# Both parts of the activations in one matmul of 512 columns: a two-block transformer kernel on one core

## The chip, the cores and the metric

The program runs on one core of one Trainium2 chip. Time is device time in microseconds (us) of that core, from launch to end of one execution; lower is better. The engines have separate instruction queues that run in order and meet at semaphores: TensorE (PE for its matmuls, PEld for its weight loads), VectorE (DVE), ScalarE (ACT), GpSimd (POOL), and SyncE (SP), which issues the DMAs of the weights.

## The reference, cut to what matters

256 tokens `x` and 256 context tokens `ctx`, all of width 2048, go through two layers of a first block and one second block. All is fp32.

```python
# first block, layers l = 0, 1
hl = xl * (1.0 + sc_l) + sh_l                       # modulation; the same for the context
parts_l = jnp.split(hl @ w_in[l], SPLIT_POINTS, axis=-1)   # cu cb cc cg q k v ag pu pg
...                                                 # conv, differential attention, pooling: gated
out_l = concatenate([y_conv, y_attn, y_pool]) @ w_out[l]
xl = _layernorm(DEEPNORM_ALPHA * xl + g_l * out_l, ln_g[l], ln_b[l])
# in the last layer the context gives k and v alone

# second block, 256 tokens
h = rms_norm(x)           # @ w_in_2: qa ka va qb kb vb f ga gb
a = attention_a @ w_proj_a_2 * sigmoid(h @ w_ga) ; b = attention_b @ w_proj_b_2 * sigmoid(h @ w_gb)
x = x + (a + b) @ w_out_2
x = x + relu(rms_norm(x) @ w_up_2) ** 2 @ w_down_2  # width 8192; then a last norm
```

(The second block's lines are condensed to what the kernel computes.) The products are wanted in nearly fp32 precision, which is why the kernel does each of them in three matmuls.

## The kernel before, in words

**Three matmuls per product.** A weight tile and an activation tile are each split in two parts, a high part (`hi`, `ah`) that holds the leading bits and a low part (`lo`, `al`) that holds the rest. A product is hi·ah + hi·al + lo·ah, three matmuls that add up in one PSUM accumulator (`mm3`, L247 to L250).

**Two kinds of product.** `lin_b` (L252) keeps 128x128 pieces of the weights stationary and moves the activations: its output is [channel, token], with as many columns as there are tokens, 512 or 256. `lin_a` (L273) keeps activations stationary and moves the weights, mostly 512 columns at a time. In both, the work goes by chunks of 256 rows of k and 512 columns of the weights (two k tiles of 128 rows). A `lin_b` call has four accumulators `acc`, one per 128 channels, from a ring of five PSUM banks: in each chunk it goes through the four blocks, and in a block through the two k tiles. After the last chunk's matmuls of a block its `consume` function takes the accumulator out of PSUM (the eviction). A full call has 8 chunks; the two projections `w_proj_a_2` and `w_proj_b_2` have 4.

**Where 256 columns move.** `lin_b` runs on 256 tokens in layer 1 for q, ag, cu, cc, cb, cg, pu and pg (10 calls, q and ag twice), and in the second block for qa, ka, qb, kb (8 calls), the gates ga and gb (8), the projections (8 calls of 4 chunks) and w_up (16), and for the small forget gate f. Layer 0, the k of layer 1 and all of `lin_a` are of another form.

**Evictions.** Copies and activations of an accumulator run on ACT (`S.copy`, `S.activation`), products with an accumulator on DVE (`V.tensor_mul`). Those of w_up are longest: relu on ACT (L1166), square on POOL (L1167), then `split` (L318): the high part by ACT (L319), the low part by DVE (L320). At the projection b: product with the gate on DVE (L1143), sum on POOL (L1144), then `split`.

**The stream of weights.** `fetch` (L171) loads a chunk by a DMA from SP into `raw`, ACT writes the high part (L186), DVE subtracts for the low part (L187). There are three buffers of each of `raw`, `hi` and `lo`; two chunks are kept ready ahead of the one in use. Between the chunks a step of background work may run: attention of the heads that are ready, normalisation, and, up to layer 1, the modulation's sums on DVE (L386).

**The order of the instructions.** It is fixed when the program is built: a scheduler takes the program's statements, by its own estimates of their durations, and lays each engine's queue out; buffers come from small rings (four of `tmp`, five of `acc`), and an instruction waits when its ring buffer is not yet free.

`Act` holds the activations' parts in slots of 2048 columns, in before two tiles, `ah` and `al`.

Of the kernel before, what the change touches and what calls it, by code (L numbers as in the profile page):

```python
# [19 lines left out]
P = 128  # L20
# [42 lines left out]
def tile_two_blocks(ctx: ExitStack, tc: tile.TileContext, a: dict, out: bass.AP, blocks: dict):  # L63
    """blocks: takes, for each weight, its blocks in the order of their loads: (part, k tile, k tiles, column, columns)."""
# [6 lines left out]
    p_ah = pool("ah", 4)  # L71
    p_al = pool("al", 4)
# [66 lines left out]
    # An entry with a function is modulation: the function takes its tile as it comes. One with an engine is split there.  # L139
# [22 lines left out]
    def block(name, *where):  # L162
        """The next block of a weight: they lie in memory in the order of their loads, each partition's part in one run."""
# [33 lines left out]
    def side():  # L197
        """Modulation at the head of the stream."""
# [30 lines left out]
    def bg_step():  # L229
        """A step after every pace[0] chunks."""  # L230
# [42 lines left out]
    def lin_a(act, tiles, consume, korder=K16, mid=None, hold=1):  # L273
        """out[tok, n]: the activations stationary, the weights moving; the last chunks (hold) one token tile at a time."""
# [21 lines left out]

    class Act:
        """n activation tiles of w tokens, their two parts, in slots of 2048 columns."""

        def __init__(self, n, w):  # L300
            self.w, self.per = w, 2048 // w
            self.t = [(p_ah.tile([P, 2048], F32R, tag="ah", name="ah"), p_al.tile([P, 2048], F32R, tag="al", name="al"))
                      for _ in range(n // self.per)]

        def __getitem__(self, kt):
            j = (kt % self.per) * self.w
            return tuple(t[:, j:j + self.w] for t in self.t[kt // self.per])

        def block(self, kt, n, sl):
            """Tokens sl of n tiles from kt on."""  # L310
            j = (kt % self.per) * self.w
            return tuple(t[:, j:j + n * self.w].rearrange("p (k t) -> p k t", t=self.w)[:, :, sl]
                         for t in self.t[kt // self.per])
# [14 lines left out]
    def set_cols(l, which, kt, n, sums):  # L328
        """Shift (0) or scale (1) columns for n k tiles: scol[l][:, kt, stream, which]."""
# [4 lines left out]
    def mod_first(which, kt, n, tags=("aT",)):  # L334
        """Layer 0 on the tensor engine: sums over each quarter of k on its own quadrant, row s of it is stream s."""
# [35 lines left out]
    def mod_side(l, nt, streams=(0, 1), wait=5):  # L371
        """Sums on each partition by the side of the products, then over the partitions."""
# [47 lines left out]
    # column offsets in w_in  # L420
# [9 lines left out]
    # the column blocks of a product that the rows' statistics wait for: the last ones are short  # L430
# [860 lines left out]
```

## Time and profile before

| | |
|---|---|
| times of three runs | 2999.6, 2999.79, 3003.39 us (median 2999.79) |
| the profiled execution: span from the first to the last instruction | 3000.6 us |
| PE busy | 2926.6 us, 98% of the span, 17762 matmuls |
| PEld busy (weight loads, beside the matmuls) | 2547.9 us, 85% |
| DVE busy | 1878.3 us, 63% |
| ACT busy | 1233.4 us, 41% |
| POOL busy | 287.0 us, 10% |
| mean granted TensorE clock | 0.990 |
| weights and other data from HBM | 527.07 MB, 177 GB/s over the span |

The profiled execution's span lies within the three run times. A busy share is an average over stages with different limits; a matmul's recorded duration is longer than the spacing of matmuls, since they overlap in the array, so the spacing of their starts is what counts. Rows of the timeline give start, duration, engine, line, operation, and in brackets how long the engine was idle before and what ended that.

### The profile page before, as it was taken

How to read it: one execution, taken by the hardware profiler on the slowest of the kernel's cores; microseconds unless marked ns; L12 is line 12 of the kernel's file. 1: busy time of each engine (PE TensorE's matmuls, PEld its weight loads, DVE VectorE, ACT ScalarE, POOL GpSimd, SP SyncE). 2: the span in 40 equal slices, each digit the busy share in tenths (PEclk: the TensorE clock that was granted, in tenths of full speed). 3: DMA queues.
4: the chain of work that ended last, by engine and by line, in shares of the span. 5: the costliest groups of instructions: out<-in, count | busy, mean ns of one | idle time of the engine just before them, and what ended most of it. 6: DMA issues, size and time to landing. Idle time of an engine off the chain costs nothing.

```text
span 3000.6 us, 44450 instructions
## 1 busy us (share of the span) xinstructions
PE 2926.6 (98%) x17762; PEld 2547.9 (85%) x17762; DVE 1878.3 (63%) x2689; ACT 1233.4 (41%) x1792; POOL 287.0 (10%) x319
## 2 busy tenths in 40 slices
PE   8999999999999999999988999999999999999998
PEld 5677777778779788888877989999989989898997
DVE  3779987887985657467565464645555545555454
ACT  3123433432312446245434454744445434344444
POOL 0001001001100411021110000000101001010011
PEclk9999999999999999999998999999999999999999
DMA  8763345446664445445654545455555555555555
GB/s 304 264 205 130 128 160 172 137 144 198 227 202 131 130 140 171 157 157 171 228 174 134 184 146 193 141 190 183 183 190 175 190 190 182 195 186 189 190 183 169
DMA packets 156456, 534.22 MB, mean 178 GB/s; under 512 B 17860, under 2 KB 21196, under 8 KB 156248
## 3 DMA queue, kind: packets, MB, share of 16 engines
q1 hardware_dynamic: 148656, 510.79, 51.0%
q0 software_dynamic: 5632, 18.36, 2.0%
q8 instruction: 139, 2.28, 0.3%
q10 hardware_dynamic: 1960, 2.22, 0.3%
q14 instruction: 69, 0.57, 0.1%
HBM read 527.07 MB, written 4.23 MB: 177 GB/s over the span
## 4 chain that ended last, share of the span: by engine, by line
PE 68%; issue 6%; DVE 4%; ACT 1%; DMA 1%; POOL 0%; ACTq 0%; POOLq 0%; DVEq 0%
PE acc L248 22%; PE acc L250 22%; PE acc L249 22%; DVE lo L187 1%; PE aux L673 1%; DVE ma L386 0%; PE aux L641 0%; PE aux L663 0%; DMA mod<-in_w_mod_dram 0%; ACT hi L186 0%; PE aux L640 0%; DVE qs L627 0%; DMA tmp<-in_invc_dram 0%; PE aux L1060 0%; ACT L1125 0%
## 5 line engine op out<-in xcount | busy, mean ns | idle before, releaser
L187 DVE TENSOR_TENSOR lo<-raw,hi 128x1024 fp32r<-128x1024 f32 x766 | 948.6, 1240 | 845.4 <-ACT hi L186 842.9
L186 ACT CAST hi<-raw 128x1024 fp32r<-128x1024 f32 x769 | 805.4, 1049 | 1388.5 <-PE acc L249 784.6
L248 PE MATMUL acc<-ah,hi 128*128 128x256 f32 (+1 forms) x3856 | 1204.6, 313 | 2.5 <-ACT p L1125 1.5
L250 PE MATMUL acc<-ah,lo 128*128 128x256 f32 (+1 forms) x3856 | 1191.8, 309 | 3.1 <-DVE lo L187 2.9
L249 PE MATMUL acc<-al,hi 128*128 128x256 f32 (+1 forms) x3856 | 1191.3, 309 | 0.0
L248 PEld LDWEIGHTS acc<-ah,hi 128*128 128x128 f32 x3856 | 737.2, 191 | 63.6 <-issue 9.9
L250 PEld LDWEIGHTS acc<-ah,lo 128*128 128x128 f32 x3856 | 736.6, 191 | 44.2 <-issue 4.1
L249 PEld LDWEIGHTS acc<-al,hi 128*128 128x128 f32 x3856 | 737.6, 191 | 36.7 <-issue 3.0
L248 PE MATMUL acc<-hi,ah 128*128 128x512 f32 (+1 forms) x1568 | 583.1, 372 | 1.5 <-ACT ah L319 1.3
L250 PE MATMUL acc<-hi,al 128*128 128x512 f32 (+1 forms) x1568 | 578.5, 369 | 0.4 <-DVE al L320 0.4
L249 PE MATMUL acc<-lo,ah 128*128 128x512 f32 (+1 forms) x1568 | 578.6, 369 | 0.0
L386 DVE SCALAR_TENSOR_TENSOR ma<-mod,cc,ma 128x512 f32<-128x512 f32 x480 | 344.3, 755 | 30.7 <-DMA mod<-in_w_mod_dram 28.8
L248 PEld LDWEIGHTS acc<-hi,ah 128*128 128x128 f32 x1568 | 296.6, 189 | 54.0 <-issue 3.2
L250 PEld LDWEIGHTS acc<-hi,al 128*128 128x128 f32 x1568 | 296.5, 189 | 50.3 <-DVE al L320 1.1
L249 PEld LDWEIGHTS acc<-lo,ah 128*128 128x128 f32 x1568 | 296.8, 189 | 48.7 <-issue 0.5
L1167 POOL TENSOR_TENSOR tmp<-tmp 128x256 f32<-128x256 f32 x64 | 57.9, 914 | 579.6 <-ACT tmp L1166 579.6
L320 DVE TENSOR_TENSOR al<-tmp,ah 128x256 fp32r<-128x256 f32 (+1 forms) x96 | 65.0, 684 | 23.8 <-ACT ah L319 21.4
L649 ACT ACTIVATE pp<-aux,small 128x512 f32<-128x512 f32 (+1 forms) x96 | 58.3, 613 | 47.6 <-DVE small L645 47.5
L513 POOL TENSOR_TENSOR tmp<-p,cs 128x256 f32<-128x256 f32 x32 | 27.7, 877 | 508.4 <-DVE p L741 262.9
L124 POOL TENSOR_TENSOR small<-small,mhalf 128x1 f32<-128x1 f32 (+2 forms) x28 | 28.3, 1011 | 484.0 <-DVE small L680 251.8
L741 DVE TENSOR_TENSOR p<-acc,p 128x512 f32<-128x512 f32 x80 | 53.2, 686 | 29.5 <-PE acc L250 29.4
L319 ACT CAST ah<-tmp 128x256 fp32r<-128x256 f32 (+1 forms) x96 | 45.1, 478 | 60.0 <-POOL tmp L1167 35.3
(205 smaller groups left out, 1582.2 us busy)
## 6 DMA issues: line engine op xcount, KB each, us to landing
raw<-in_w_in_dram SPq DMA_DIRECT2D x384, 512.0 KB, 3.6
mod<-in_w_mod_dram SPq DMA_DIRECT2D x158, 512.0 KB, 4.3
raw<-in_w_up_dram SPq DMA_DIRECT2D x128, 512.0 KB, 3.3
raw<-in_w_down_dram SPq DMA_DIRECT2D x128, 512.0 KB, 3.5
raw<-in_w_out_dram SPq DMA_DIRECT2D x96, 512.0 KB, 4.4
mod<-in_w_mod_dram SPq DMA_DIRECT2D x68, 256.0 KB, 5.4
raw<-in_w_proj_a_dram SPq DMA_DIRECT2D x16, 512.0 KB, 3.2
raw<-in_w_proj_b_dram SPq DMA_DIRECT2D x16, 512.0 KB, 3.7
```

The source lines that it names most:

```text
L186: S.copy(hi, raw)
L187: (fn or V).tensor_sub(lo, raw, hi)
L248: mm(ps, lh, rh, start=start, stop=False)
L249: mm(ps, lh, rl, start=False, stop=False)
L250: mm(ps, ll, rh, start=False, stop=stop)
L319: S.copy(h, src)
L320: V.tensor_sub(lo, src, h)
L386: V.scalar_tensor_tensor(st[s], raw[:, kk, :], cc2[:, k, s:s + 1], st[s], op0=ALU.mult, op1=ALU.add)
L649: S.activation(t, ps[i][:, :nk], AF.Exp, bias=nm[:, i:i + 1], scale=QK_SCALE, accum_out=sums[:, i:i + 1])
L673: mm(po[:, o * P:(o + 1) * P], t[:, kt * P:(kt + 1) * P], vt[kt, g][:, hc * P:(hc + 1) * P], start=kt == 0, stop=kt == nk // P - 1)
L741: V.tensor_add(t, ps, t)
L1167: G.tensor_mul(t, t, t)
```

## The change

A `lin_b` call on 256 tokens joins the first two of the three matmuls: the stationary high part of the weights meets both parts of the activations at once, as 512 moving columns (256 of `ah`, then 256 of `al`), and writes them side by side into one PSUM bank of 512 columns. The third matmul, lo·ah, still has 256 columns and adds into the first half. So the accumulator holds two halves whose sum is wanted. `consume` gets a view that puts the two halves of a token next to each other, and the sum is formed on eviction by a DVE reduction of pairs: straight into the destination where a copy stood (`put`), else into a `tmp` tile on which the former operation then works (`val`). Both parts of the activations now lie in one tile, so that one access pattern reaches them. Calls on 512 tokens and `lin_a` stay as they were.

```diff
@@ lin_b
+        fold = 2 * ntok == 512
...
-                    mm3(p[:w, :ntok], hi[:, kk, c:c + w], lo[:, kk, c:c + w], ah[:, tok], al[:, tok],
-                        k0 == korder[0] and kk == 0, last and kk == nk - 1)
+                    start, stop = k0 == korder[0] and kk == 0, last and kk == nk - 1
+                    if fold:
+                        mm(p[:w, :].rearrange("p (a t) -> p a t", a=2), hi[:, kk, c:c + w], act.both(k0 + kk, tok),
+                           start=start, stop=False)
+                        mm(p[:w, :ntok], lo[:, kk, c:c + w], ah[:, tok], start=False, stop=stop)
+                    else:
+                        mm3(p[:w, :ntok], hi[:, kk, c:c + w], lo[:, kk, c:c + w], ah[:, tok], al[:, tok], start, stop)
                 if last:
-                    consume(c // P, p[:w, :ntok])
+                    consume(c // P, (p[:w].rearrange("p (a t) -> p t a", a=2),) if fold else p[:w, :ntok])
...
+    def put(t, ps):
+        if isinstance(ps, tuple):
+            V.reduce_sum(t, ps[0], axis=AX.X)
+        else:
+            S.copy(t, ps)
+    def val(ps):
+        if not isinstance(ps, tuple):
+            return ps
+        t = tmp(T)[:ps[0].shape[0]]
+        V.reduce_sum(t, ps[0], axis=AX.X)
+        return t
...
     class Act:
-            self.t = [(p_ah.tile([P, 2048], F32R, tag="ah", name="ah"), p_al.tile([P, 2048], F32R, tag="al", name="al"))
-                      for _ in range(n // self.per)]
+            self.t = [p_act.tile([P, 2, 2048], F32R, tag="act", name="act") for _ in range(n // self.per)]
...
+        def both(self, kt, tok):
+            j = (kt % self.per) * self.w
+            return self.t[kt // self.per][:, :, j + tok.start:j + tok.stop]
...
@@ evictions, three of them
-                S.copy(t, ps)
+                put(t, ps)
...
-            V.tensor_mul(t, ps, t)
+            V.tensor_mul(t, val(ps), t)
             G.tensor_add(t, t, sga[4 * j + b])
             split(mg[4 * j + b], t)
...
-                S.activation(t, ps, AF.Relu)
+                S.activation(t, val(ps), AF.Relu)
```

The built program shows it on two engines. First TensorE, at the start of a w_up call: the rows of its first block's two k tiles, before.

```order
L248 MATMUL acc_21329<-ah_20949,hi_21251 128x256
L249 MATMUL acc_21329<-al_20950,hi_21251 128x256
L250 MATMUL acc_21329<-ah_20949,lo_21252 128x256
L248 MATMUL acc_21329<-ah_20949,hi_21251 128x256
L249 MATMUL acc_21329<-al_20950,hi_21251 128x256
L250 MATMUL acc_21329<-ah_20949,lo_21252 128x256
```

The same call and block of the changed program, and the first tile of the next block.

```order
L267 MATMUL acc_19520<-act_19200,hi_19450 128x512
L269 MATMUL acc_19520<-act_19200,lo_19451 128x256
L267 MATMUL acc_19520<-act_19200,hi_19450 128x512
L269 MATMUL acc_19520<-act_19200,lo_19451 128x256
L267 MATMUL acc_19521<-act_19200,hi_19450 128x512
```

Six matmuls of 256 columns have become two of 512 and two of 256; over the program there are 2944 such pairs that became one matmul.

Second, VectorE at the end of the first w_up call, before: from the low part of the next call's second chunk (`lo_21282`) on.

```order
L187 TENSOR_TENSOR lo_21282<-raw_21279,hi_21281 128x1024
L320 TENSOR_TENSOR al_20990<-tmp_21291,ah_20989 128x256
L320 TENSOR_TENSOR al_20990<-tmp_21302,ah_20989 128x256
L187 TENSOR_TENSOR lo_21336<-raw_21333,hi_21335 128x1024
L320 TENSOR_TENSOR al_20990<-tmp_21313,ah_20989 128x256
L320 TENSOR_TENSOR al_20990<-tmp_21324,ah_20989 128x256
L187 TENSOR_TENSOR lo_21366<-raw_21363,hi_21365 128x1024
```

The same place of the changed program: `lo_19473`, `lo_19527` and `lo_19549` are the next call's second, third and fourth chunk.

```order
L315 TENSOR_REDUCE tmp_19481<-acc_19240 128x256
L186 TENSOR_TENSOR lo_19473<-raw_19470,hi_19472 128x1024
L315 TENSOR_REDUCE tmp_19492<-acc_19241 128x256
L340 TENSOR_TENSOR act_19238<-tmp_19480,act_19238 128x256
L315 TENSOR_REDUCE tmp_19503<-acc_19242 128x256
L186 TENSOR_TENSOR lo_19527<-raw_19524,hi_19526 128x1024
L340 TENSOR_TENSOR act_19238<-tmp_19491,act_19238 128x256
L315 TENSOR_REDUCE tmp_19514<-acc_19243 128x256
L340 TENSOR_TENSOR act_19238<-tmp_19502,act_19238 128x256
L186 TENSOR_TENSOR lo_19549<-raw_19546,hi_19548 128x1024
L340 TENSOR_TENSOR act_19238<-tmp_19513,act_19238 128x256
```

Four reductions stand between the weights' low parts and the activations' low parts, one per accumulator.

Third, VectorE at the end of the first call of projection b, before: products with the gate (L1143), low parts of the result (L320), and of the next call's second, third and fourth chunk (L187).

```order
L1143 TENSOR_TENSOR p32_18887<-acc_18911,p32_18887 128x256
L187 TENSOR_TENSOR lo_19008<-raw_19005,hi_19007 128x1024
L320 TENSOR_TENSOR al_18658<-p32_18887,ah_18657 128x256
L1143 TENSOR_TENSOR p32_18887<-acc_18912,p32_18887 128x256
L1143 TENSOR_TENSOR p32_18902<-acc_18913,p32_18902 128x256
L1143 TENSOR_TENSOR p32_18902<-acc_18914,p32_18902 128x256
L187 TENSOR_TENSOR lo_19058<-raw_19055,hi_19057 128x1024
L320 TENSOR_TENSOR al_18658<-p32_18887,ah_18657 128x256
L320 TENSOR_TENSOR al_18658<-p32_18902,ah_18657 128x256 x2
L187 TENSOR_TENSOR lo_19088<-raw_19085,hi_19087 128x1024
```

The same place of the changed program, where the product with the gate is L1166 and the low part of the third chunk is `lo_17549`.

```order
L315 TENSOR_REDUCE tmp_17506<-acc_17426 128x256
L186 TENSOR_TENSOR lo_17499<-raw_17496,hi_17498 128x1024
L1166 TENSOR_TENSOR p32_17400<-tmp_17506,p32_17400 128x256
L315 TENSOR_REDUCE tmp_17516<-acc_17427 128x256
L315 TENSOR_REDUCE tmp_17526<-acc_17428 128x256
L340 TENSOR_TENSOR act_17230<-p32_17400,act_17230 128x256
L1166 TENSOR_TENSOR p32_17400<-tmp_17516,p32_17400 128x256
L1166 TENSOR_TENSOR p32_17415<-tmp_17526,p32_17415 128x256
L315 TENSOR_REDUCE tmp_17536<-acc_17429 128x256
L340 TENSOR_TENSOR act_17230<-p32_17400,act_17230 128x256
L1166 TENSOR_TENSOR p32_17415<-tmp_17536,p32_17415 128x256
L186 TENSOR_TENSOR lo_17549<-raw_17546,hi_17548 128x1024
```

The third chunk's low part has moved from behind the last product and one low part of the result to behind the last product and two of them, with four reductions more ahead of it.

## Rows read from the trace of the kernel before

**Rows 1.** The page's part 1: busy time (share of the span) and instructions.
```profile
span 3000.6 us, 44450 instructions
PE 2926.6 (98%) x17762; PEld 2547.9 (85%) x17762; DVE 1878.3 (63%) x2689; ACT 1233.4 (41%) x1792; POOL 287.0 (10%) x319
```

**Rows 2.** Waits of PE, the longest first: total us, times, longest.
```profile
PE aux L983 <- ACT p L975: 13.0, 2, 9.3
PE aux L983 <- DVE small L813: 12.6, 1, 12.6
```

**Rows 3.** Groups of instructions, forms apart: xcount | busy us, mean ns.
```profile
L249 PE MATMUL acc<-al,hi 128*128 128x256 f32 x2944 | 835.0, 284 | 0.0
```

**Rows 4.** Timeline of PE, first and last of 51 matmuls in a row.
```profile
1999.92 0.28 PE L248 MATMUL acc<-ah,hi 128*128 128x256 f32 x1
...
2005.92 0.28 PE L250 MATMUL acc<-ah,lo 128*128 128x256 f32 x1
```

**Rows 5.** Timeline of PE in a `lin_a` call, first and last of 55 matmuls.
```profile
2419.59 0.39 PE L250 MATMUL acc<-hi,al 128*128 128x512 f32 x1
...
2431.82 0.39 PE L250 MATMUL acc<-hi,al 128*128 128x512 f32 x1
```

**Rows 6.** DVE reductions by line: xcount, ns min/median/max, first and last start, forms.
```profile
L642 DVE TENSOR_REDUCE small<-aux x96: 410/680/693, 284.6 to 1395.1; 128x1 f32<-128x512 f32 x64, 128x1 f32<-128x256 f32 x32
...
L361 DVE TENSOR_REDUCE small<-aux x8: 168/178/192, 16.1 to 224.7; 128x4 f32<-128x16 f32 x4, 128x8 f32<-128x32 f32 x4
```

**Rows 7.** Timeline of DVE in the attention of layer 1.
```profile
1122.32 1.29 DVE L642 TENSOR_REDUCE small<-aux 128x1 f32<-128x512 f32 x2
```

**Rows 8.** Timeline of DVE at the end of a projection b call.
```profile
2072.57 1.07 DVE L1143 TENSOR_TENSOR p<-acc,p 128x256 f32<-128x256 f32 x3
2073.57 1.31 DVE L187 TENSOR_TENSOR lo<-raw,hi 128x1024 fp32r<-128x1024 f32 x1
```

**Rows 9.** Timeline of ACT at the end of a w_up call.
```profile
2317.46 0.38 ACT L1166 ACTIVATE tmp<-acc 128x256 f32<-128x256 f32 x1
2318.07 0.39 ACT L1166 ACTIVATE tmp<-acc 128x256 f32<-128x256 f32 x1 [0.23 <-PE acc L250]
2319.31 0.41 ACT L319 CAST ah<-tmp 128x256 fp32r<-128x256 f32 x1 [0.86 <-POOL tmp L1167]
```

**Rows 10.** POOL and DVE steps behind evictions, by line, as in rows 6.
```profile
L1167 POOL TENSOR_TENSOR tmp<-tmp x64: 607/838/1369, 2294.9 to 2905.9; 128x256 f32<-128x256 f32 x64
...
L1144 POOL TENSOR_TENSOR p<-p,p x16: 737/1256/1722, 2070.1 to 2179.4; 128x256 f32<-128x256 f32 x16
...
L320 DVE TENSOR_TENSOR al<-tmp,ah x96: 424/552/1816, 21.0 to 2907.5; 128x256 fp32r<-128x256 f32 x64, 128x512 fp32r<-128x512 f32 x32
```

**Rows 11.** Timeline of DVE at the end of layer 1's first q call.
```profile
1102.77 0.45 DVE L511 STREAM_SHUFFLE tmp<-p 128x256 f32<-128x256 f32 x1
...
1103.46 1.31 DVE L512 TENSOR_TENSOR tmp<-tmp,cs 128x256 f32<-128x256 f32 x2
1104.70 0.75 DVE L514 TENSOR_TENSOR p<-tmp 128x256 f32<-128x256 f32 x2
```

**Rows 12.** Windows: us, busy PE PEld DVE ACT POOL, PEclk, DMA share, GB/s.
```profile
1104.00:1139.00 35.00, 32.07 (x216) 27.92 (x215) 33.50 (x47) 25.85 (x42) 10.82 (x9) 0.95 0.59 185
1139.00:1173.00 34.00, 31.95 (x226) 27.67 (x225) 29.98 (x53) 22.87 (x42) 6.04 (x3) 1.00 0.53 184
1319.00:1351.00 32.00, 29.97 (x209) 25.51 (x208) 31.45 (x47) 21.25 (x38) 11.04 (x8) 1.00 0.59 186
1351.00:1384.00 33.00, 30.92 (x228) 27.46 (x227) 29.61 (x53) 21.39 (x39) 4.89 (x5) 1.00 0.52 170
1885.00:1917.00 32.00, 31.83 (x257) 31.26 (x255) 22.20 (x63) 21.29 (x36) 0.00 (x0) 1.00 0.41 144
...
2300.00:2400.00 100.00, 100.00 (x700) 94.05 (x699) 51.75 (x52) 45.76 (x61) 11.06 (x13) 1.00 0.55 188
```

More of the change, by code (lines that the diff above doesn't have):

```diff
@@ L70, in tile_two_blocks @@
     p_wl = pool("wl", 3)
-    p_ah = pool("ah", 4)
-    p_al = pool("al", 4)
+    p_act = pool("act", 4)
     p32 = pool("p32", 20)
@@ L301, in __init__ @@
             self.w, self.per = w, 2048 // w
-            self.t = [(p_ah.tile([P, 2048], F32R, tag="ah", name="ah"), p_al.tile([P, 2048], F32R, tag="al", name="al"))
-                      for _ in range(n // self.per)]
+            self.t = [p_act.tile([P, 2, 2048], F32R, tag="act", name="act") for _ in range(n // self.per)]
         def __getitem__(self, kt):
             j = (kt % self.per) * self.w
-            return tuple(t[:, j:j + self.w] for t in self.t[kt // self.per])
-        def block(self, kt, n, sl):
+            t = self.t[kt // self.per]
+            return t[:, 0, j:j + self.w], t[:, 1, j:j + self.w]
+        def both(self, kt, tok):
             j = (kt % self.per) * self.w
-            return tuple(t[:, j:j + n * self.w].rearrange("p (k t) -> p k t", t=self.w)[:, :, sl]
-                         for t in self.t[kt // self.per])
+            return self.t[kt // self.per][:, :, j + tok.start:j + tok.stop]
     new_act = Act
@@ L533, in c @@
                 t = qt_[4 * g + b] = pair("q", 4 * g + b)
-                S.copy(t, ps)
+                put(t, ps)
                 rope(t[:, X] if both else t)
@@ L539, in c @@
             def c(b, ps):
-                S.activation(y_tile(4 + 4 * g + b), ps, AF.Silu)
+                S.activation(y_tile(4 + 4 * g + b), val(ps), AF.Silu)
             lin_b(hT, qs, c)
@@ L547, in c @@
             def c(b, ps):
-                S.copy(y_tile(b), ps)
+                put(y_tile(b), ps)
             lin_b(hT, qs, c)
@@ L553, in c @@
                 v = tmp(NT)
-                V.tensor_mul(v, ps, Y[b])
+                V.tensor_mul(v, val(ps), Y[b])
                 w = lambda i: smc("cw", l * 12 + b * 3 + i)
@@ L564, in c @@
             def c(b, ps):
-                V.tensor_mul(Y[b], ps, Y[b])
+                V.tensor_mul(Y[b], val(ps), Y[b])
             lin_b(hT, qs, c)
@@ L570, in c @@
                 s = tmp(NT)
-                S.activation(s, ps, AF.Silu)
+                S.activation(s, val(ps), AF.Silu)
                 G.tensor_mul(Y[b], Y[b], s)
@@ L582, in c @@
                 G.memset(u[:, :, 264:272], 0.0)
-                S.copy(u[:, :, 8:264], sh(ps))
+                if isinstance(ps, tuple):
+                    put(u[:, 0, 8:264], ps)
+                else:
+                    S.copy(u[:, :, 8:264], sh(ps))
                 w = WINDOWS[b]
@@ L608, in c @@
                 s = tmp(NT)
-                S.activation(s, ps, AF.Silu)
+                S.activation(s, val(ps), AF.Silu)
                 G.tensor_mul(Y[12 + b], Y[12 + b], s)
@@ L1007, in c @@
             if n[0] == "q":
-                S.activation(t, ps, AF.Copy, scale=HD_SCALE)
+                S.activation(t, val(ps), AF.Copy, scale=HD_SCALE)
             else:
-                S.copy(t, ps)
+                put(t, ps)
         lin_b(hn, TK, c)
@@ L1027, in c @@
             f, e, fone = tmp(T), tmp(T), tmp(T)
-            V.tensor_scalar(f[:NH], ps, sm[:NH, SM["bf"][0]:SM["bf"][1]], None, op0=ALU.add)
+            V.tensor_scalar(f[:NH], val(ps), sm[:NH, SM["bf"][0]:SM["bf"][1]], None, op0=ALU.add)
             S.activation(e[:NH], f[:NH], AF.Abs)
@@ L1124, in c @@
             sga[4 * j + b] = t = pair("sga", 4 * j + b)
-            S.activation(t, ps, AF.Sigmoid)
+            S.activation(t, val(ps), AF.Sigmoid)
         lin_b(hn, TK, c)
@@ L1128, in c @@
         def c(b, ps):
-            V.tensor_mul(sga[4 * j + b], ps, sga[4 * j + b])
+            V.tensor_mul(sga[4 * j + b], val(ps), sga[4 * j + b])
         lin_b(aA, TK, c, korder=K8)
@@ L1137, in c @@
             sgb[b] = pair("sgb", b)
-            S.activation(sgb[b], ps, AF.Sigmoid)
+            S.activation(sgb[b], val(ps), AF.Sigmoid)
         lin_b(hn, TK, c)
```

## The prediction

> **What bounds the kernel now.** I read the page's busy shares first, then PE's waits, then the spacing of matmul starts, and last the busy time of VectorE by stretches. PE is busy 98% of 3000.6 us [rows 1], and its longest waits belong to the two norms and last 13 us each [rows 2]. None is for an accumulator or a weight part, so in most of the program PE sets the pace and whatever shortens its stream shortens the run. The exceptions are the attention stretches of layer 1, where VectorE is busy 29.6 to 33.5 us of 32 to 35 while PE idles 2 to 3 us in each [rows 12]. Outside them, as in w_up and w_down, VectorE is busy 52% and PE all the time [rows 12].
>
> **What the change removes from PE.** A matmul's recorded length (284 ns at 256 columns [rows 3]) is not its price, since starts are closer. From the first to the last of 51 matmuls of 256 columns are 50 steps in 6.00 us, 120.0 ns each [rows 4]; from the first to the last of 55 of 512 columns are 54 steps in 12.23 us, 226.5 ns each [rows 5]. Two matmuls of 256 cost 240.0, one of 512 costs 226.5. The saving is 13.5 ns for each of 2944 pairs [rows 3], 39.7 us in all. (The forget gate has 16 pairs more, worth 0.2 us, which I leave out.) This is the whole gain. No row shows a moving operand in two pieces 8 KB apart. Its price lies between 226.5 (as one piece) and 240.0 (as two matmuls); I take 226.5, since the 512 columns stream into one bank as in the rows.
>
> The Trainium skill (TensorE: Matmul & The Clock Gate, Back-to-back issue gap) gives a warm gap of N/2.4 + 2.5 ns. By it, folding two matmuls would save 2.5 ns, 7.4 us in all, and not 39.7. The trace disagrees: both spacings exceed their columns' time at 2.4 GHz (106.7 and 213.3 ns) by 13.2 to 13.3 ns. I keep the measured steps; that the fold brings far less is a rival below.
>
> **What it adds to VectorE.** There are 50 calls with four evictions each, and one for f: 201 reductions, each of 512 inputs to 256 outputs. No row has this shape. By inputs, a reduction of 512 from PSUM takes 683 ns and one of 256 takes 410 [rows 6]; the lower end is 410, if pairs went at the rate of outputs. For the upper end, the small strided reductions go from 168 ns (16 inputs, 4 outputs) to 192 (32 and 8): 24 ns, of which 16 inputs at 1.07 ns (from 410 to 683 for 256) explain 17. So 7 ns go to 4 outputs; 256 outputs would add 0.46 us, giving 1.14. I take 0.68, the nearest in inputs. Back to back each takes less, 0.61 (two end within 1.29 us [rows 7]), and a product 0.33 (three in 1.00 us [rows 8]). That makes 123 us of new VectorE work. Nearly all lies beside PE, which must not be taken for free: the reduction waits for PE, the next chunks' low parts queue behind it on VectorE, and PE waits for those and for the freed accumulator. ACT loses 32 copies, which nobody waits for; the DMAs' order stays, and the faster chunk (2.77 us instead of 2.88) asks for 4% more than a DMA share of 0.55 [rows 12].
>
> **Deadlines at the end of a call.** Let t = 0 be the start of the last chunk. A block is two pairs of 226.5 + 120.0, so 0.69 us, and a chunk 2.77. A block's eviction may start about 0.2 us after its end (0.28 us of length against 0.12 of spacing, and the handoff). Of five accumulators the next call uses the spare first, so it needs the old blocks 0, 1 and 2 free at 3.46, 4.16 and 4.85. Its second, third and fourth chunk must be ready at 5.5, 8.3 and 11.1.
>
> *w_up* (16 calls). On VectorE: reduction 0 at 0.90, low part of chunk 2 (1.15 us net) at 1.51, reduction 1 at 2.66, done 3.34, in time for 4.16. Then the low part of the result, which waits for relu, square and high part: 0.38, about 0.95 (between 0.61 and 1.37) and 0.41 us, with handoffs, from 1.6 to 3.5 [rows 9, 10]. It ends at 3.9, so reduction 2 is done at 4.6, 0.25 us before its deadline. The chain of the next results runs on until 12; chunk 4's low part is ready at 10.4, needed at 11.1. I book nothing here, but the margin is 0.25 us.
>
> *q and k, quiet gates, projection a*: reductions 0 to 2 end at 1.6, 3.3 and 4.0 to 4.4. Nothing.
>
> *Projection b* (4 calls). In the new order the low part of chunk 3 stands behind four reductions, four products and two low parts that wait for POOL. Following it: product 0 at 2.66, reductions 1 and 2 at 3.0 and 3.6, low part 0 at 4.85 (POOL's sum takes 1.26 [rows 10]), products 1 and 2, reduction 3 at 5.9, low part 1 at 7.4, product 3 at 7.8, chunk 3 from 8.15 to 9.4. PE wants it at 8.3 plus one hi matmul, 8.5. That is 0.8 us late; L320 and L1144 stretch to 1.8 and 1.7 us where they run together [rows 10], so I take 1.2 (bounds 0 and 2.0): 4.8 us.
>
> The product with the gate has now both inputs in SBUF. The Trainium skill (SBUF — State Buffer, Who interferes with whom) says such a VectorE instruction and a GpSimd one that reads SBUF exclude each other for a whole instruction. By it the new product may wait out a sum of 1.26 us, an estimate that would put the four calls at 2.0 us each; no row has this pair, and the bound of 2.0 covers it.
>
> *Gates a under attention* (2 calls): VectorE is at 22.2 of 32 us [rows 12] with chains that wait for ACT, and 2.4 us more are due. I take 1.0 each (0 to 2): 2.0.
>
> *Layer 1* (10 calls). In each of the two stretches with ag and cu, and ag and cb, eight reductions add 4.9 us to a VectorE that has 5.5 and 3.9 us idle [rows 12], mostly in pieces too short to use. Bounds are 0 and 4.9; I take 3.0 each, 6.0. At q, a rotation stands between the reductions: after reduction 1 at 3.0 come product 0 (0.65), shuffle 1 (0.35), sum 0 (0.37) and product 1 (0.65) [rows 11], so reduction 2 starts at about 5.5, is done at 6.2, and its accumulator was due at 4.85: 1.3 us (0 to 2.3), twice 2.6. The four other calls get 0.6 each (0 to 1.5): 2.4. Together 11.0.
>
> **Sum.** 39.7 - 4.8 - 2.0 - 11.0 = 21.9 us less. Against the profiled span, 3000.6 - 21.9 = 2978.7; the median of the runs is 0.8 below that span, and from it comes 2977.9. I forecast 2978.
>
> **Rivals.** A measurement of this kernel can tell 0.2% (6.0 us) from no change.
>
> *All reductions hide.* Idle time on VectorE takes them up, as it does now in w_up: 2999.8 - 39.7 = 2960. Against it speak the filled attention stretches; for it, that three chunks of slack have absorbed delays so far.
>
> *The stalls eat the gain.* All upper bounds together (layer 1: 9.8 + 4.6 + 6.0, gates 4, projection b 8) make 32.4, so 2992.5; some w_up slips of 0.3 us bring it to about 2998, no change.
>
> *Pairs are slow on VectorE: slower than before.* If a reduction takes 1.14 us, reduction 2 of every w_up call is done at 5.7 instead of 4.85, 0.9 us late (14.4); the 18 plain calls are 0.45 late (8.1); projection b gets 1.4 more a call (5.6), the gates under attention 1.8 together, and layer 1 some 60% of 40 times 0.46 (11.0). That adds 40.9 to the 17.8 already booked: 2999.8 - 39.7 + 58.7 = 3019. It decides from about 0.92 us a reduction, where gain and loss are equal. For it speak the strided rows, against it that 7 ns in 24 is little to build on.
>
> *The two pieces cost as two.* If the joined matmul takes 240 ns, the gain is nothing and the stalls remain: 2999.8 + 17.8 = 3018. By the skill's 2.5 ns a pair it would be 3010. Little speaks for it.
>
> **Chances.** Forecast 50%, with its own range of 2968 to 2992; all hidden 20%; gain eaten 10%; slow pairs 14%; no gain on PE 6%. Faster by over 0.2%: the first two and a third of the third, 0.73. Within: the rest of the third and the mildest of the slow-pair cases, 0.11. Slower: 0.16. The range of 2957 to 3006 leaves out the two slow cases, except their mildest.
>
> **What would show it.** The joined matmuls should start 226 ns, the lo ones 120 ns before their successor. Reductions on DVE should last 0.65 to 0.72 us; over 0.9 would prove the slow-pair rival. PE's waits should name the low part of the weights after projection b and reductions in layer 1, and almost nothing in w_up. PE should do a w_up call in 22.2 us instead of 23.0. I am wrong if w_up calls are longer than that, or if layer 1's ten calls lose much more than 11 us.

## The result, and the profile after

The changed kernel takes 2967.2 us (median of 4 runs, 2966.4 to 2968.3) against 2999.8 for the kernel before, a ratio of 0.989 (95% interval 0.988 to 0.991). That is 32.5 us less; I had forecast 21.8 less, 2978. The time lies within the stated range (2957 to 3006) and 0.8 us below the likeliest case's own range. The direction was right and the size a third too small. The sum behind it was worse than that: two large terms were wrong, in opposite directions, so that the time fell inside the range is partly luck.

The page's head after, to be held against [rows 1]:

```profile
span 2964.5 us, 38716 instructions
PE 2899.2 (98%) x14802; PEld 2382.4 (80%) x14802; DVE 1978.0 (67%) x2890; ACT 1213.7 (41%) x1750; POOL 296.9 (10%) x319
```

PE has 2960 matmuls fewer, DVE 201 instructions and 99.7 us more. PE still sets the pace. Its first waits after, to be held against [rows 2]:

```profile
PE aux L1006 <- ACT p L998: 13.0, 2, 9.3
PE aux L1006 <- DVE small L836: 12.6, 1, 12.6
PE aux L919 <- ACT p L912: 5.9, 1, 5.9
PE aux L367 <- DVE csil L133: 5.4, 1, 5.4
PE acc L269 <- DVE lo L186: 4.6, 4, 1.3
```

The norms' waits (first two rows) are the same to a tenth. The last row is the largest on `acc`: four waits for the weights' low part, all in layer 1's two ag calls (2.9 us in two waits before, in ag and cu). No wait for a reduction itself is among the long ones.

The cleanest reading comes from PE's starts. Both kernels issue the same products, so the start of each call's first matmul can be laid side by side. The gain of each group of calls, from the two profiles (spans 3000.6 and 2964.5):

| calls with 256 tokens | pairs | ideal (13.5 ns a pair) | forecast, net | profiles |
|---|---|---|---|---|
| layer 1, ten calls | 640 | 8.6 | -2.4 | 16.1 |
| block 2: q, k, f | 512 | 6.9 | 6.9 | 3.3 |
| gates a (two under attention) | 256 | 3.5 | 1.5 | 4.8 |
| projections, gates b | 512 | 6.9 | 2.1 | 6.3 |
| w_up, 16 calls | 1024 | 13.8 | 13.8 | 6.1 |
| all the rest | | 0 | 0 | -0.5 |
| sum | 2944 | 39.7 | 21.9 | 36.1 |

Three things stand out: w_up and q/k gave under half of their ideal though PE waits there for 0.7 us in all; the projections and gates b gave nearly all of it; layer 1 gave twice its ideal. (The profiles differ by 36.1 us and the medians by 32.5. The changed kernel's profiled run was 0.8 us faster than its median, and a time is 1.8 to 1.9 us longer than its span in the later runs, which would put the profiled run of before some 2.6 us above its own.)

**The joined stream has two rhythms.** From the last quarter of the last gate a call into the second call of projection a no step is a wait, and the timeline of PE gives 63 pairs from the first to the last of these rows (start, length in us):

```profile
1960.40 0.39 PE L267 MATMUL acc<-act,hi 128*128 128x512 f32 x1
...
1982.24 0.40 PE L267 MATMUL acc<-act,hi 128*128 128x512 f32 x1
```

21.84 us for 63 pairs is 346.7 ns, the 226.5 + 120.0 that I had booked [rows 4, 5]. The same in a w_up call, also without a wait:

```profile
2444.15 0.40 PE L267 MATMUL acc<-act,hi 128*128 128x512 f32 x1
...
2466.41 0.40 PE L267 MATMUL acc<-act,hi 128*128 128x512 f32 x1
```

22.26 us for 63 pairs is 353.3 ns. A call of 64 pairs takes 22.61 us then instead of 22.19 (before 23.04), at a granted clock of 1.00 in both. A stretch keeps its rhythm until something interrupts the stream: the row of 512-column calls before w_up leaves it in the slow one every time; after the attention it runs in the fast one for 115 us, until a wait of 0.15 us at 2049.2 tips it over. In the next gates b call it is back in the fast one. Summed over all steps that are no waits, the slow rhythm costs about 14 us.

The Trainium skill (TensorE: Matmul & The Clock Gate, Back-to-back issue gap) has an isolated gap of N/2.4 + 2.5 ns for a matmul of N columns at the 2.4 GHz level; added for 512 and 256 columns, that is an estimate of 325 ns for such a pair. The measured 346.7 and 353.3 both disagree, as the rows of before had.

### The profile page after: what moved, and what is told of

The parts are those of the page before. It is cut to its first block, busy times and chain, and to the rows that moved or that the text cites. A ratio compares the mean times of both kernels' runs of the same rounds, so it can differ in the third digit from the quotient of the medians.

```text
span 2964.5 us, 38716 instructions
## 1 busy us (share of the span) xinstructions
PE 2899.2 (98%) x14802; PEld 2382.4 (80%) x14802; DVE 1978.0 (67%) x2890; ACT 1213.7 (41%) x1750; POOL 296.9 (10%) x319
## 4 chain that ended last, share of the span: by engine, by line
PE 71%; issue 5%; DVE 2%; DMA 1%; ACT 1%; POOL 0%; ACTq 0%; POOLq 0%; DVEq 0%
PE acc L267 22%; PE acc L269 11%; PE acc L247 11%; PE acc L249 11%; PE acc L248 11%; PE aux L696 1%; PE aux L664 1%; PE aux L663 0%; DVE lo L186 0%; PE aux L686 0%; PE aux L1083 0%; ACT hi L185 0%; DVE p L952 0%; DMA raw<-in_w_in_dram 0%; POOL small L123 0%
## 5 line engine op out<-in xcount | busy, mean ns | idle before, releaser
L267 PE MATMUL acc<-act,hi 128*128 128x512 f32 x2960 | 1052.1, 400 | 0.6 <-DVE qs L306 0.6
L269 PE MATMUL acc<-act,lo 128*128 128x256 f32 x2960 | 830.7, 281 | 4.6 <-DVE lo L186 4.6
L267 PEld LDWEIGHTS acc<-act,hi 128*128 128x128 f32 x2960 | 555.3, 188 | 139.8 <-issue 3.5
L247 PE MATMUL acc<-hi,act 128*128 128x512 f32 (+1 forms) x1568 | 582.7, 372 | 1.5 <-ACT act L339 1.3
L248 PE MATMUL acc<-lo,act 128*128 128x512 f32 (+1 forms) x1568 | 578.9, 369 | 0.2 <-DVE lo L186 0.2
L249 PE MATMUL acc<-hi,act 128*128 128x512 f32 (+1 forms) x1568 | 578.4, 369 | 0.5 <-DVE act L340 0.5
L269 PEld LDWEIGHTS acc<-act,lo 128*128 128x128 f32 x2960 | 558.3, 189 | 8.2 <-DVE lo L186 6.3
L247 PE MATMUL acc<-act,hi 128*128 128x512 f32 x896 | 359.2, 401 | 0.5 <-DVE p L764 0.5
L249 PE MATMUL acc<-act,lo 128*128 128x512 f32 x896 | 351.7, 393 | 0.0
L248 PE MATMUL acc<-act,hi 128*128 128x512 f32 x896 | 351.6, 392 | 0.0
L247 PEld LDWEIGHTS acc<-hi,act 128*128 128x128 f32 x1568 | 296.4, 189 | 54.4 <-issue 3.2
L248 PEld LDWEIGHTS acc<-lo,act 128*128 128x128 f32 x1568 | 296.7, 189 | 50.1 <-DVE lo L186 1.4
L249 PEld LDWEIGHTS acc<-hi,act 128*128 128x128 f32 x1568 | 296.4, 189 | 49.9 <-DVE act L340 1.1
L247 PEld LDWEIGHTS acc<-act,hi 128*128 128x128 f32 x896 | 168.8, 188 | 55.3 <-issue 9.4
L249 PEld LDWEIGHTS acc<-act,lo 128*128 128x128 f32 x896 | 168.8, 188 | 39.3 <-issue 3.6
L248 PEld LDWEIGHTS acc<-act,hi 128*128 128x128 f32 x896 | 168.9, 189 | 35.6 <-issue 3.0
L315 DVE TENSOR_REDUCE tmp<-acc 128x256 f32<-128x512 f32 x169 | 112.9, 684 | 52.2 <-PE acc L269 52.2
```

The costliest lines, as they stand in the source:

```text
L247: mm(ps, lh, rh, start=start, stop=False)
L248: mm(ps, lh, rl, start=False, stop=False)
L249: mm(ps, ll, rh, start=False, stop=stop)
L267: mm(p[:w, :].rearrange("p (a t) -> p a t", a=2), hi[:, kk, c:c + w], act.both(k0 + kk, tok), start=start, stop=False)
L269: mm(p[:w, :ntok], lo[:, kk, c:c + w], ah[:, tok], start=False, stop=stop)
L315: V.reduce_sum(t, ps[0], axis=AX.X)
```

## The experiments

**The kernel before, profiled again.** No edit.

> The kernel before, unchanged, to be profiled a second time. In its first profile the last call of layer 1 (the gate of the pooled branch) took 32.97 us, with one wait of 4.77 us for a table that comes by DMA, and TensorE's half clock after it; after the change that call takes 26.40 us. Theory A, that this wait is luck of one transfer: the call takes 26 to 29 us in the new profile, and the span is 3 to 5 us below the 3000.6 of the first. Theory B, that the order of the kernel before makes the wait: 32 to 34 us again and a span near 3000. The time is 2999.8 by both.

The median was 3000.5 (2995.8 to 3004.1, 10 runs), the profiled span 2995.0. Layer 1's last call took 27.85 us instead of 32.97, cu 38.9 instead of 37.1, ag 30.5 instead of 33.4; outside layer 1 nearly every call was the same to 0.03 us. So the kernel before scatters by 8 us over ten runs (the changed one by 2 over four), and between the two profiles the difference lies in layer 1. Theory A is right for the one profile, but the wait is no single accident: with cu's copies moved, below, that call took 32.6 us again. Layer 1's ten calls took 306.1 and 299.9 us in the two profiles, and 290.0 after: of the 16.1 in the table up to 6 are the first profile's. The stretch ahead of layer 1's q, which no edit below touches, took 1078.5 to 1082.6 us in the profiles of the changed kernel and its variants; so profiles are compared call by call, and 2 to 3 us between medians of four runs prove little.

**The fold left out in layer 1.**

```
-        fold = 2 * ntok == 512
+        fold = 2 * ntok == 512 and act.w == 256
```

> The changed kernel, with the joined matmul left out in layer 1 (its ten calls run as before; block 2 stays changed). The joined matmuls of layer 1 are worth 8.6 us less 3.2 for their slow rhythm. Theory A, that the change also takes waits out of layer 1 because ScalarE no longer stands in its queue waiting for TensorE's accumulators: this kernel is about 10 us slower than the changed one, 2977. Theory B, that layer 1 gets only the stream's gain and the rest of what the profile showed there was luck: 2967.2 + 5.4 = 2972.6. My prediction (layer 1 loses 2.4 us net): 2964.8.

2979.2 us, ratio to before 0.993 (0.991 to 0.994). Layer 1 is worth 11.9 us by the times, free of the first profile's luck. 8.6 less 3.2 for the rhythm comes from the stream; the other 6.5 is what theory A is about, waits that went away (2977 expected, so somewhat more than that). My -2.4 is refuted.

**The copies on VectorE, without the fold.** In the kernel before, layer 1's q, cu and pu leave the accumulator through VectorE.

```
-                S.copy(y_tile(b), ps)
+                (S.copy if both else V.tensor_copy)(y_tile(b), ps)    # the same in do_q and do_pu
```

> The kernel before, with one part of the change alone: in layer 1 the copies out of the accumulators in q, cu and pu (16 copies) go to VectorE instead of ScalarE; matmuls as before. Theory A, that ScalarE's queue is freed from waiting for TensorE and the softmax chains run earlier: the waits in front of the attention matmuls in the call cu fall from 3.65 us (waits there and before its own matmuls) to about 1.2, the time to about 2997. Theory B, that this copy's place does not matter: 2999.8 and the waits as before; if the 16 copies delay the low parts on VectorE, up to 3002.

2994.3 us, 0.998 (0.997 to 0.999): 6.2 us less than before, with the stream of matmuls unchanged, and more than theory A's 2997 said. cu took 34.2 us, the last call 28.1. So the move of the evictions off ScalarE, which I had booked at nothing ("ACT loses 32 copies, which nobody waits for"), is worth as much as layer 1's whole stream gain. The next four runs look for the copies that matter.

**cu's copies alone on VectorE, in the kernel before** (the edit above in do_cu only).

> The kernel before, with only the four copies of layer 1's call cu on VectorE. Moving 16 copies (q, cu and pu) brought the time from 3000.5 to 2994.3 us. If it is cu, whose copies stand on ScalarE among the exponentials of the attention (theory A1): cu takes 34 to 35 us instead of 37 to 39, and the time is 2996 to 2997. If it is pu, whose results wait for a table by DMA (theory A2): cu as before and 3000.

3001.0 us, 1.000 (0.999 to 1.001); cu 37.3, the last call 32.6. Not cu.

**cu, pu and q back through ScalarE, in the changed kernel**, one at a time: VectorE still reads the accumulator, ScalarE copies the sum.

```
-                put(y_tile(b), ps)
+                S.copy(y_tile(b), val(ps))        # cu_act; the same in do_pu (pu_act) and do_q (q_act)
```

> The changed kernel with cu's four results brought to their place by ScalarE: VectorE adds the halves, ScalarE copies. By theory A1 cu, now 32.9 us, gets 2 to 4 us longer and the time is 2969 to 2971. If ScalarE's share in cu does not matter: 2967.2.

> The changed kernel with pu's four results brought to their place by ScalarE after VectorE has added the halves. In front of the pooled products TensorE waited 5.1, 2.4 and 3.2 us in the three profiles with this copy on ScalarE, and 0.9 us in two with it on VectorE. By theory A2 the waits are 2 to 5 us again and the time is 2969 to 2972; if that was the transfers' luck, 2967.2 and waits of about 1 us.

> The changed kernel with q's eight results of layer 1 brought to their place by ScalarE after VectorE has added the halves. In the kernel before, ScalarE's copies of q stood between its casts of the weights' high part and of the attention's operands at the start of call ag; with the copies on VectorE the calls ag and cu of the first attention took together 66.3 us (copies moved alone) and 64.9 (the changed kernel), with them on ScalarE 69.4 to 70.5 in three profiles of the kernel before and one of the changed kernel without layer 1. Theory A3 (the copies of q are what did it): ag and cu take 68 to 70 us together, and the time is 2970 to 2973. Rival (it is the whole layout of work on VectorE, and no single copy): 65 to 66 us and 2967.

cu_act took 2966.2 us and q_act 2966.0, the changed kernel's time within their spread of 3 to 4 us; cu took 32.9 us in cu_act, as in the changed kernel, and ag and cu together 66.5 in q_act (64.9 in the changed kernel), while the second attention was 1.4 us shorter. Theories A1 and A3 fall. (In all three runs the sum passes through a `tmp` buffer that the changed kernel does not use there, so they change more than who copies.) pu_act took 2971.9, 4.6 more. In its profile the last call took 29.7 us against 26.4, and 1.2 us more is the slow rhythm, which stayed through the later gates b and projections b. So theory A2's time came: where pu's copy runs matters. pu's block waits for a table that ScalarE's queue fetches by DMA. The waits of DVE for it over layer 1's last three calls (us, times, longest), one fence per kernel: before, before again, changed, and changed with pu through ScalarE.

```profile
DVE tmp L596 <- DMA tmp<-in_invc_dram: 5.2, 3, 4.6
```

```profile
DVE tmp L596 <- DMA tmp<-in_invc_dram: 2.3, 1, 2.3
```

```profile
DVE tmp L619 <- DMA tmp<-in_invc_dram: 1.1, 1, 1.1
```

```profile
DVE tmp L619 <- DMA tmp<-in_invc_dram: 3.4, 2, 3.2
```

On PE those arrive as 5.1, 2.4 and 0.9 us in front of the pooled products; in pu_act PE waits 3.9 us for an accumulator behind them instead. But the two waits are not the same, and a table issued late behind the copy is not what the kernel before shows. In pu_act it is the first of four tables that DVE waits 3.2 us for; it was issued at 1433.5, in the changed kernel at 1411.1. In the kernel before the first one is early too (1418.5), and the last is late, after it was issued: 8.7 us from its issue to its use (6.4, 7.7 and 6.6 in the three other profiles with pu's accumulators read by ScalarE).

```profile
1447.90 0.33 ACTq L593 DMA_DIRECT2D tmp<-in_invc_dram  x1
```

```profile
1456.57 0.42 DVE L596 TENSOR_TENSOR tmp<-qs,tmp 128x256 f32<-128x256 f32 x1 [4.59 <-DMA tmp<-in_invc_dram]
```

In the changed kernel it is used 5.35 us after its issue, without a wait. What else moved is GpSimd's queue. In the kernel before it stands idle for 18 us until pu's block frees a buffer, and then issues ten loads of 256 KB within 6 us, just before and behind the last table's issue:

```profile
1446.04 0.54 POOL L1054 DMA_DIRECT2D qs<-in_cs_dram  x1 [18.07 <-DVE qs L589]
...
1447.42 2.12 POOL L821 DMA_DIRECT2D p<-in_ln_g_dram  x4
1449.53 2.12 POOL L821 DMA_DIRECT2D p<-in_ln_b_dram  x4
```

In the changed kernel eight of the ten go out ahead of the last three tables:

```profile
1417.71 2.12 POOL L844 DMA_DIRECT2D p<-in_ln_g_dram  x4
1419.82 2.23 POOL L844 DMA_DIRECT2D p<-in_ln_b_dram  x4
```

So it is in all fourteen profiles: beside the last table in the four where ScalarE reads pu's accumulators, ahead of the last three tables in the ten where VectorE does, pu_act among them. That these loads make the table late is argued from this and from a DMA share of 1.03 in the wait (first row below); no run moved them alone.

A long wait is then paid twice. These windows of the kernel before (us, busy PE PEld DVE ACT POOL, PEclk, DMA share, GB/s) hold the wait of 4.5 us for the table, what follows it, and what follows a wait of 1.8 us for a low part in the first ag call:

```profile
1453.00:1457.00 4.00, 0.32 (x3) 0.11 (x1) 0.43 (x2) 1.34 (x3) 0.54 (x1) 0.89 1.03 406
1458.50:1463.00 4.50, 4.50 (x22) 4.41 (x21) 2.64 (x6) 0.77 (x2) 2.86 (x6) 0.50 1.00 327
...
1132.00:1135.00 3.00, 3.00 (x16) 3.00 (x15) 3.00 (x4) 2.95 (x4) 0.82 (x1) 0.50 0.57 187
```

The granted clock is 0.50, the 1.2 GHz level, and 256-column matmuls start every 213 ns there instead of 120: 1.7 and 1.4 us more. In the changed kernel no wait for a low part is longer than 1.3 us, and the clock over the first ag call is 1.00 (0.95 before [rows 12]).

**The two parts of an activation side by side.**

```
-            self.t = [p_act.tile([P, 2, 2048], F32R, ...
+            self.t = [p_act.tile([P, self.per, 2, w], F32R, ...        # both(): one run of 512 columns in block 2
```

> The changed kernel with the two parts of an activation tile side by side, so that in block 2 the 512 columns of the joined matmul are one contiguous piece of 2 KB (in layer 1 two pieces 2 KB apart instead of 8 KB). In the changed kernel a pair of matmuls takes 346.7 ns in some stretches and 353.3 in others, which costs 14 us in all. Theory A, that the slow rhythm comes from the alternation of a long and a short matmul: both rhythms as before, about 2967. Theory B, that it comes from the moving operand in two pieces: 346.7 ns everywhere in block 2, about 2967 - 11 = 2956.

2967.7 us, 0.989 (0.987 to 0.990), w_up calls 22.61 as before. The rhythm is not from the moving operand in two pieces, and my rival that the pieces cost as two is refuted at both layouts.

**Another order of the matmuls.** Within a block first the two of 512 columns, then the two of 256 (lo_pairs); within a chunk the eight of 512, then the eight of 256 (lo_last, where the new loop stands behind all four blocks, except in a call's last chunk).

```
                 for kk in range(nk):
...
-                        mm(p[:w, :ntok], lo[:, kk, c:c + w], ah[:, tok], start=False, stop=stop)
+                for kk in range(nk if fold else 0):
+                    mm(p[:w, :ntok], lo[:, kk, c:c + w], act[k0 + kk][0][:, tok], start=False,
+                       stop=last and kk == nk - 1)
```

> The changed kernel with another order inside an accumulator's block: the two joined matmuls of 512 columns first, then the two of 256 with the low part. Half as many changes of size. If the 6.6 ns of the slow rhythm belong to each change of size (theory A), half the 14 us come back: 2960. If a block always takes its columns' steps of 226.5 and 120.0 once no size changes in between (theory B), w_up calls go to 22.2 us and the time to 2954. If the rhythm has to do with something else (theory C), 2967.

> The changed kernel with all eight joined matmuls of a chunk first and its eight low-part matmuls behind them (in the last chunk of a call block by block, two and two). One change of size in 16 matmuls instead of each. Theory A (6.6 ns at each change of size): nearly all of the 14 us come back, 2954. Besides, the low part of the weights is needed 1.8 us later, so the waits for it (four of 4.6 us in all in layer 1) go: 2950. Theory C (rhythm has another cause): 2963, by the waits alone.

lo_pairs: 2958.9 us, 0.986 (0.985 to 0.988), the fastest kernel here. From the first to the last row are 31 blocks of two pairs in a w_up call:

```profile
2444.51 0.63 PE L267 MATMUL acc<-act,hi 128*128 128x512 f32 x2
...
2466.10 0.62 PE L267 MATMUL acc<-act,hi 128*128 128x512 f32 x2
```

21.59 us make 696.5 ns a block, 348.2 a pair, and all undisturbed calls take 22.28 to 22.31 us, whatever ran before. So the order removes the slow rhythm and settles a little above the fast one. Half of 6.6 ns for half the changes of size (theory A) would be 350.0; lo_last, with an eighth of them, still needs 22.31 to 22.37. So a price for each change of size does not describe it, and neither does B's 22.2 to the last tenth. What makes the two rhythms I cannot say: the trace shows that each weight load starts with the matmul before it in both.

lo_last: 2969.9 us, 0.990 (0.988 to 0.991), slower than lo_pairs through one new wait: the second to fourth w_up call of each quarter takes 23.25 us. DVE shows why, at the end of a w_up call:

```profile
2463.76 1.28 DVE L320 TENSOR_REDUCE tmp<-acc 128x256 f32<-128x512 f32 x2
2466.17 1.23 DVE L186 TENSOR_TENSOR lo<-raw,hi 128x1024 fp32r<-128x1024 f32 x1 [1.13 <-ACT hi L185]
2467.32 0.83 DVE L345 TENSOR_TENSOR act<-tmp,act 128x256 fp32r<-128x256 f32 x1
2468.34 0.42 DVE L345 TENSOR_TENSOR act<-tmp,act 128x256 fp32r<-128x256 f32 x1 [0.19 <-ACT act L344]
2468.68 1.28 DVE L320 TENSOR_REDUCE tmp<-acc 128x256 f32<-128x512 f32 x2
```

The build laid the third reduction behind a low part and two results, and PE waits 0.7 us for the accumulator. 12 such calls at 0.95 us are the 11 us to lo_pairs.

**w_up's reductions twice.**

```
+                v = val(ps)
+                V.reduce_sum(v, ps[0], axis=AX.X)
-                S.activation(t, val(ps), AF.Relu)
+                S.activation(t, v, AF.Relu)
```

> The changed kernel with every reduction of w_up done twice (64 more, 0.61 to 0.68 us each; same result). It tests the margin of 0.25 us that the prediction worked out for w_up. By that theory reduction 2 of a call ends 1.0 to 1.6 us after its deadline, and each of 16 calls gets 0.8 to 1.5 us longer: 2980 to 2991. By the rival, that VectorE has 37% idle time in w_up and takes anything up, 2967.

2975.4 us, 8.1 more. Only the calls behind another w_up call pay, 12 of 16, with 0.54 to 0.98 us each. VectorE is busy 61% in w_up and does not take up 0.6 us at that place: the margin is real. The price was smaller than expected, since four of the calls have no successor that waits, and in this build a late block stands behind parts of the next chunk.

**Reductions replaced by copies of the first half.**

```
-        V.reduce_sum(t, ps[0], axis=AX.X)
+        V.tensor_copy(t, ps[0][:, :, 0])        # in put and val
```

> The changed kernel with the 201 reductions replaced by copies of the first 256 columns (it leaves out the addition of the high part times the activations' low part). A copy of 256 takes about 0.41 us instead of 0.68, so VectorE has some 50 us less to do. If reductions cost nothing on the path any more (theory A), 2967, within 2. If they still hold up layer 1, where TensorE waits 4.6 us for low parts and 2 to 3 us more in each ag call (theory B), 2961 to 2964.

2969.7 us, 0.990 (0.988 to 0.991): not less, though each eviction fell from 683 to 417 ns. Theory B is half right, though: PE's waits for low parts in the two ag calls fell from 4.6 to 2.2 us, and those calls by 1.3 and 1.6. But cu came out at 35.6 us, cb at 34.8 and the last call at 27.6 in this layout, 2.7, 1.0 and 1.2 more than in the changed kernel, which I did not follow up; layer 1 as a whole took 2.1 us more. So shorter evictions bring nothing in sum, which is not the same as that the reductions cost nothing anywhere.

## Why the prediction was right and wrong

**The stream, 13.5 ns a pair: right where the rhythm is fast, half of it where it is slow.** "This is the whole gain", I wrote, from two steps that were each measured in streams of one size. The trace of before has no stream that alternates sizes, and the sum of steps held only as a lower end: 226.5 + 120.0 was met at 346.7 and missed at 353.3. I had bounded the joined matmul between 226.5 and 240.0; 353.3 - 120.0 = 233.3 lies inside that, but the range was not carried further than one rival. Mis-sized by about 14 us. My own test (wrong "if w_up calls are longer than that", 22.2 us) came true for this reason, and not through waits.

**The reductions: right.** By the page's groups the 169 of L315 last 684 ns on average, against 0.68 booked and 0.92 as the point where slow pairs decide. The slow-pair rival is out.

```profile
L315 DVE TENSOR_REDUCE tmp<-acc 128x256 f32<-128x512 f32 x169 | 112.9, 684 | 52.2 <-PE acc L269 52.2
```

**w_up, no stall and a margin of 0.25 us: right.** The last chunk of this call starts at 2441.32. DVE then:

```profile
2442.23 0.69 DVE L315 TENSOR_REDUCE tmp<-acc 128x256 f32<-128x512 f32 x1 [1.35 <-PE acc L269]
2442.84 1.22 DVE L186 TENSOR_TENSOR lo<-raw,hi 128x1024 fp32r<-128x1024 f32 x1
2443.97 0.68 DVE L315 TENSOR_REDUCE tmp<-acc 128x256 f32<-128x512 f32 x1
2445.00 0.42 DVE L340 TENSOR_TENSOR act<-tmp,act 128x256 fp32r<-128x256 f32 x1 [0.34 <-ACT act L339]
2445.34 0.68 DVE L315 TENSOR_REDUCE tmp<-acc 128x256 f32<-128x512 f32 x1
```

The reductions start 0.9, 2.65 and 4.0 us after it (worked out: 0.90, 2.66 and about 3.9), and the third ends at 4.70 against a deadline of 4.85 (4.95 in the slow rhythm). lo_last and double_red show what a miss costs.

**Projection b, 4.8 us lost: wrong, nothing lost.** The order was as I followed it, but from the first low part of the result on every step came 0.4 to 0.9 us earlier. The last chunk of this call starts at 2040.83:

```profile
2043.80 1.28 DVE L315 TENSOR_REDUCE tmp<-acc 128x256 f32<-128x512 f32 x2
2045.24 0.42 DVE L340 TENSOR_TENSOR act<-p,act 128x256 fp32r<-128x256 f32 x1 [0.16 <-ACT act L339]
2045.58 0.75 DVE L1166 TENSOR_TENSOR p<-tmp,p 128x256 f32<-128x256 f32 x2
2046.25 0.68 DVE L315 TENSOR_REDUCE tmp<-acc 128x256 f32<-128x512 f32 x1
2047.40 0.51 DVE L340 TENSOR_TENSOR act<-p,act 128x256 fp32r<-128x256 f32 x1 [0.47 <-ACT act L339]
2047.83 0.41 DVE L1166 TENSOR_TENSOR p<-tmp,p 128x256 f32<-128x256 f32 x1
2048.17 1.21 DVE L186 TENSOR_TENSOR lo<-raw,hi 128x1024 fp32r<-128x1024 f32 x1
```

The low part of chunk 3 ends at 8.55 us, where I had 9.4, and PE wants it at 8.5. POOL's sum for the first result took 0.73 us where I had taken the median of before, 1.26 [rows 10]. That median mixes two cases: in the kernel before a sum beside products or the result's low part took 0.7 to 0.9 us and one beside the weights' low part 1.6 to 1.7, and the first sum of each call stood beside a low part. In the new order it meets reductions:

```profile
2044.03 0.73 POOL L1167 TENSOR_TENSOR p<-p,p 128x256 f32<-128x256 f32 x1 [145.84 <-DVE p L1166]
```

Sums beside a low part still take 1.65 to 1.77. The 1.8 us that I read in [rows 10] for L320 belongs to low parts of 512 columns, 986 to 1031 us into the program, and to no projection. Of the 16 products, now with both inputs in SBUF, 15 took 0.41 to 0.42 us and one, beside a sum and a low part, 0.96; none waited out a sum of 1.26. The wait of PE is 0.05 to 0.15 us.

**Layer 1, 11.0 us lost: the failed step.** Instead 6.5 us came back on top of the stream. Three parts of it:

- *The price of a fuller VectorE* (6.0 us for the two attentions). DVE is now busy 31.4 of 32 and 32.4 of 33 us in the windows that answer to [rows 12], and PE works more of the time, not less:

```profile
1102.00:1134.00 32.00, 29.70 (x147) 22.12 (x146) 31.42 (x50) 22.25 (x36) 11.56 (x10) 1.00 0.52 174
1134.00:1167.00 33.00, 32.99 (x178) 25.75 (x176) 32.40 (x59) 23.54 (x42) 5.60 (x3) 1.00 0.60 202
```

  Summed lengths overlap, so a DVE that looks full can still take work. The reductions do delay low parts in the ag calls (4.6 us of waits, 2.2 in half_red), but with shorter ones the four attention calls took 131.5 us together, and with the reductions 130.8.
- *q, 1.3 us a call.* The third reduction came late, nearly as I put it (5.15 to 5.8 us after the last chunk's start, where I had 5.5 to 6.2, and the deadline was 4.85), but nobody waited: the build issues the block that needs its accumulator behind the next chunk's first blocks. PE's queue of the changed kernel at that place:

```
L269 MATMUL acc_9051<-act_8060,lo_9000 128x256
L267 MATMUL acc_9052<-act_8060,hi_8999 128x512
L267 MATMUL acc_9054<-act_8060,hi_8977 128x512
L269 MATMUL acc_9054<-act_8060,lo_8978 128x256
```

  acc_9054 is the fourth block; it takes the first chunk's weights (8977, 8978) after four matmuls with 9051 and one with 9052 have used the second's (8999, 9000). I worked the deadline out for source order.
- *What I booked at nothing.* The evictions' move off ScalarE brought 6.2 us by itself, about half of it in the last call (28.1 us, against 27.9, 32.6 and 33.0 in three profiles with pu's copy on ScalarE) and half in the two attentions. In the last call the table came late in the kernel before, with the clock's fall on top, and in time after. In the attentions the four calls took 137.2 to 138.3 us in four profiles with q's evictions on ScalarE, 134.8 with q, cu and pu moved alone, and 130.8 in the changed kernel; PE's waits for ScalarE's exponentials in them were 4.0 to 5.9, 4.4 and 1.0 us. Why is not settled: it is neither cu's eviction nor ScalarE's time for copying q. That q's accumulators are read by VectorE is left; moving them alone was not tried.

**Gates a under attention, 2.0 us lost: wrong in sign.** Beyond the stream, at the rhythm they ran in, they gained about 1.6 us. In all three profiles of before and its variant with cu moved, PE waits there for accumulators that ScalarE's sigmoid has yet to read:

```profile
PE acc L248 <- ACT p L1125: 1.5, 2, 1.1
```

After, with VectorE as the reader, PE has no such wait in these calls. I had asked how late VectorE would free the accumulators, and not how late ScalarE did it already.

**The rivals.** All hidden, 2960, came nearest in mechanism: PE waits little for what the reductions delay. Its time was missed through the rhythm, about 14 us more, and through the waits that went away in layer 1 and at the gates a, about 8 us less. The other three are refuted by the rows above. Summed anew, 39.7 less 14 for the rhythm, plus 6.5 in layer 1 and 1.6 at the gates a, makes 33.8 us; measured were 32.5.

## What to carry to other kernels

When matmuls of two sizes alternate, don't add up steps measured in streams of one size: try the order within a block, which here was worth 8 us and cost nothing. An eviction moved between engines changes more than the two queues: the build lays out all of them anew, and here GpSimd's loads moved as well, from beside the last table to ahead of the tables. List what stands behind it in every queue, DMAs above all. And work out a deadline from the order that was built, not from the source.

## What the hardware showed that was not expected

One stream of instructions ran at 346.7 or 353.3 ns a pair at the same granted clock, and stayed at one of them until it was interrupted; in the run with half reductions no such interruption came after the gates a, and it kept 346.7 through both projections. A wait of 1.8 us was followed by 3 us at the 1.2 GHz level, while waits of up to 1.3 us in the changed kernel's two ag calls were not. A sum of 256 columns on GpSimd took 0.73 us beside reductions on VectorE and 1.65 beside the subtraction that makes the weights' low part.
